# Convolution history kept as a partial sum, and decay and gate comparisons that read PSUM

## The chip, the cores and the metric

The kernel runs on one core of a Trainium2 chip. The metric is the device time of one execution in microseconds (us). Three runs of the kernel before took 3788.0, 3789.68 and 3792.01 us; the median, 3789.68 us, is what the prediction is about. Below, PE is the matrix engine (TensorE), PEld its weight loads, DVE is VectorE, ACT is ScalarE, POOL is GpSimd and SP the engine that issues most DMAs. SBUF is the working memory, PSUM the accumulators that PE writes; POOL reads SBUF alone here.

## The reference

One decoder layer over 1024 tokens of width 1024. Cut to what matters:

```
proj = rms_norm(x) @ w_in      -> z, xbc, dt, u, v, q, gates
xbc  = silu(conv(xbc))         # causal depthwise convolution, 4 taps, 1536 channels
       conv: y[t] = b + w3*x[t] + w2*x[t-1] + w1*x[t-2] + w0*x[t-3]
branch A (SSD), per chunk of 128 tokens and head:
       L[s,l] = exp(a_cs[l] - a_cs[s]) where l >= s, else 0
       y_diag = (L * (B C^T)) applied to x*dt ;  a state is carried from chunk to chunk
branches B (spatial gate) and C (attention into 256 memory tokens), merged by gates, out projection
x = x + PEER(rms_norm(x)):
       per token 8 heads choose 16 of 16384 experts (i, j), i, j < 128, with softmax gates
       out = sum over chosen e of gate_e * gelu(u_e . x) * v_e
```

## The kernel before

**Blocks.** Tokens are worked through in three blocks of 256, 256 and 512 (`BLOCKS`). `mixer(b, ...)` does the three branches of a block. For blocks 0 and 1 the chosen experts' rows are gathered from memory row by row (`gathered`): per token tile and slot one indirect DMA issued by POOL (L793), and one DVE operation of 128x1024 (L803 for u, L810 for v). For block 2 all experts are computed densely (`dense`), with a matrix of gates, one value per token and expert, that `gate_matrix` builds beforehand. The gathers run all through the kernel beside the other work. Most matmuls take three passes (L187 to L189, `mm3`) on a high and a low half of each operand; `unit` fetches a weight tile, ACT makes its high half (L160), and POOL, or DVE for some, makes the low half by a subtraction of two SBUF tiles (L161).

**Convolution (`conv_tile`).** Features stand on the 128 partitions, tokens along the free dimension; there are 12 tiles a block. PE leaves the projection in a PSUM tile (`mm_ps`, four buffers). ACT writes tap 3 and the bias to the tile `ac` in SBUF (L297). For each of the other taps DVE does two operations: L300 adds the shifted projection, read from PSUM, to `ac`; L302 adds, on the first 3, 2 or 1 tokens, the last tokens of the block before, kept in SBUF in `hist`. Then ACT copies the block's last three tokens from PSUM to `hist` (L304) and applies Silu (L306); after L304 the PSUM tile is free. PE turns some results to token order (L310, into `tp_ps`, two buffers).

**Decay product (`chunk_a`).** Per chunk PE makes two B C^T products in one `tp_ps` tile (L413), ACT copies them to `cbs` in SBUF (L416, one buffer), PE and ACT make four tiles of exponentials (L419 to L427), and DVE multiplies each by `cbs` (L428).

**Gate matrix (`gate_matrix`).** For each of four token tiles, PE turns expert numbers j, gates and expert numbers i into one `tp_ps` tile (L817); ACT copies j and the gates to `tr` in fp32 (L819) and i to `ti` in bf16 (L821). Then, 32 times for four tokens each (called a quad below; 128 in all): DVE compares `iota4` with i into `eq` in bf16 (L827) and `iota` with j into `oj` in fp32 (L829), both 128x512; POOL multiplies three tokens of `eq` by the gate (L833, 128x384), ACT the fourth (L836); PE multiplies the two (L839, four matmuls); ACT copies the result out (L841); each eight quads SP writes a stage to memory (L843). `eq`, `oj`, `oi` and the activations of `dense` share 22 buffers (`d2`).

**Order.** The program is written in one order; a scheduler lays the instructions of each engine out by priorities, and each engine runs its own list in order. Some gathers are tied to weight units by `pace`.

Of the kernel before, what the change touches and what calls it, by code (L numbers as in the profile page):

```python
# [21 lines left out]
T = 512  # L22
TT = T // P
BLOCKS = ((0, 256), (256, 256), (512, 512))
# [5 lines left out]
NXBC = 12  # L30
# [12 lines left out]
POOL_G = 3  # L43
# [15 lines left out]
def layer_kernel(ctx, tc, a, out_d):  # L59
    nc = tc.nc  # L60
# [28 lines left out]
    def d2(dp, dt=F32):  # L89
        return dp.tile([P, T], dt, tag="d2", name="d2", bufs=NDP)  # L90
# [4 lines left out]
    def col(v, n):  # L95
        return v[:, n:n + 1]
# [30 lines left out]
    a_neg = const.tile([P, 16], F32, name="a_neg")  # L127
    nc.scalar.activation(a_neg, rows[:, RW_ALOG:RW_ALOG + 16], AF.Exp)
    nc.vector.tensor_scalar(a_neg, a_neg, -1.0, None, op0=ALU.mult)
    hist = const.tile([P, NXBC, 3], F32, name="hist")  # L130
    nc.vector.memset(hist, 0.0)
    prev = const.tile([P, D], F32, name="prev")

    x2_d = drm.tile([SEQ, D], F32, name="x2_d")
# [154 lines left out]
                                           op0=ALU.mult, op1=ALU.subtract)  # L289
        return hT  # L290

    def conv_tile(f, hT, dst, turned):
        T = hT[0].shape[-1]
        ps = feat(a["win_a"][FA_XBC + f], hT)
        cw = PK_CONVW + f * 4
        ac = t2()[:, :T]
        nc.scalar.activation(ac, ps, AF.Identity, bias=col(pk, PK_CONVB + f), scale=col(pk, cw + 3))  # L297
        for j in range(3):
            s = 3 - j
            nc.vector.scalar_tensor_tensor(ac[:, s:T], ps[:, 0:T - s], col(pk, cw + j), ac[:, s:T],  # L300
                                           op0=ALU.mult, op1=ALU.add)
            nc.vector.scalar_tensor_tensor(ac[:, 0:s], hist[:, f, j:3], col(pk, cw + j), ac[:, 0:s],  # L302
                                           op0=ALU.mult, op1=ALU.add)
        nc.scalar.copy(hist[:, f, :], ps[:, T - 3:T])  # L304
        src = ac if dst is None else dst
        nc.scalar.activation(src, ac, AF.Silu)  # L306
        if turned is not None:
            tp = tp_ps()
            for c in range(T // P):
                nc.tensor.transpose(tp[:, c * P:(c + 1) * P], src[:, c * P:(c + 1) * P], ident)  # L310
            nc.scalar.copy(turned, tp[:, :T].rearrange("p (c d) -> p c d", c=T // P))
# [4 lines left out]
    def mixer(b, hT, lmt=None):  # L316
# [7 lines left out]

        xy = b16()[:, :TT * D].rearrange("p (c d) -> p c d", c=TT)
        for f in range(4):
            conv_tile(f, hT, None, xy[:, :, f * P:(f + 1) * P])
            yield "conv"

        bc = a16()  # L330
# [12 lines left out]
            mm3(fps[0:16, :], hi[:, k, :], lo[:, k, :], hT[0][:, k, :], hT[1][:, k, :], k == 0, k == KD - 1)  # L343
        dtT = tT()
        nc.scalar.copy(dtT[0:16, :], fps[0:16, :])
        conv_tile(4, hT, None, xy[:, :, 4 * P:5 * P])
        yield "conv"
        dps = tp_ps()
        for t in range(TT):
# [20 lines left out]
        nc.vector.scalar_tensor_tensor(dt, dr, 0.0, pol, op0=ALU.max, op1=ALU.add)  # L370
        adt = s64()
        nc.vector.tensor_tensor(adt, dt, a_neg[:, None, :].to_broadcast([P, TT, 16]), op=ALU.mult)
        conv_tile(8, hT, bcT[:, 0, :], btok[:, :, 0:P])
        yield "conv"
        cps = tp_ps()
        adt_f = adt.rearrange("p c h -> p (c h)")
# [12 lines left out]
        nc.scalar.activation(cdec, cps[:, 64:64 + NS].rearrange("p (c h) -> p c h", c=TT), AF.Exp)  # L389

        for f in (9, 10, 11):
            conv_tile(f, hT, bcT[:, f - 8, :], btok[:, :, (f - 8) * P:(f - 7) * P] if f < 10 else None)
            yield "conv"
        for f in (5, 6, 7):
            conv_tile(f, hT, None, xy[:, :, f * P:(f + 1) * P])
            yield "conv"

        def gate(n, f):
# [10 lines left out]
        def chunk_a(c):  # L409
            cb = tp_ps()  # L410
            cs = slice(c * P, (c + 1) * P)
            for g in range(2):
                nc.tensor.matmul(cb[:, g * P:(g + 1) * P], lhsT=bcT[:, g, cs], rhs=bcT[:, 2 + g, cs],  # L413
                                 start=True, stop=True)
            cbs = sml.tile([P, 2, P], F32, tag="cbs", name="cbs", bufs=1)
            nc.scalar.copy(cbs, cb[:, 0:256].rearrange("p (g l) -> p g l", g=2))  # L416
            for x in range(4):
                seg = mm_ps()
                nc.tensor.matmul(seg, lhsT=identb, rhs=maskb[:, None, :].to_broadcast([P, 4, P]), start=True, stop=False)  # L419
                for j in range(4):  # L420
                    h = x * 4 + j
                    nc.tensor.matmul(seg[:, j * P:(j + 1) * P], lhsT=adt[:, c, h:h + 1].to_broadcast([P, P]),
                                     rhs=triu, start=False, stop=(j == 3))
                lm = lmt[:, (c + 1) % 2, x]
                for j in range(4):
                    h = x * 4 + j
                    nc.scalar.activation(lm[:, j, :], seg[:, j * P:(j + 1) * P], AF.Exp, bias=nacs[:, c, h:h + 1])  # L427
                nc.vector.tensor_tensor(lm, lm, cbs[:, x // 2, None, :].to_broadcast([P, 4, P]), op=ALU.mult)  # L428
# [385 lines left out]
    def gate_matrix(t, i_f, j_f, gt, dp):  # L814
        tp = tp_ps()
        for n, v in enumerate((j_f, gt, i_f)):
            nc.tensor.transpose(tp[:, n * P:(n + 1) * P], v, ident)  # L817
        tr = sml.tile([P, 2, P], F32, tag="cbs", name="tr", bufs=1)
        nc.scalar.copy(tr, tp[:, 0:256].rearrange("p (n t) -> p n t", n=2))  # L819
        ti = sml.tile([P, P], BF16, tag="tri", name="tri", bufs=1)  # L820
        nc.scalar.copy(ti, tp[:, 256:384])  # L821
        for s in range(P // STG):
            stage = a16().rearrange("p (i t) -> p i t", t=STG)
            for q in range(STG // 4):
                m0 = s * STG + q * 4
                eq = d2(dp, BF16).rearrange("p (i t) -> p i t", t=4)
                nc.vector.tensor_tensor(eq, iota4, ti[:, None, m0:m0 + 4].to_broadcast([P, P, 4]), op=ALU.is_equal)  # L827
                oj = d2(dp).rearrange("p (t i) -> p t i", t=4)
                nc.vector.tensor_tensor(oj, iota[:, None, :].to_broadcast([P, 4, P]),  # L829
                                        tr[:, 0, m0:m0 + 4, None].to_broadcast([P, 4, P]), op=ALU.is_equal)  # L830
                oi = d2(dp).rearrange("p (t i) -> p t i", t=4)
                e4 = eq.rearrange("p i t -> p t i")
                nc.gpsimd.tensor_tensor(oi[:, 0:POOL_G], e4[:, 0:POOL_G],  # L833
                                        tr[:, 1, m0:m0 + POOL_G, None].to_broadcast([P, POOL_G, P]), op=ALU.mult)
                for u in range(POOL_G, 4):
                    nc.scalar.activation(oi[:, u], e4[:, u], AF.Copy, scale=tr[:, 1, m0 + u:m0 + u + 1])  # L836
                ps = mm_ps()
                for u in range(4):
                    nc.tensor.matmul(ps[:, u * P:(u + 1) * P], lhsT=oj[:, u, :], rhs=oi[:, u, :],  # L839
                                     start=True, stop=True)  # L840
                nc.scalar.copy(stage[:, :, q * 4:q * 4 + 4].rearrange("p i t -> p t i"),  # L841
                               ps.rearrange("p (t i) -> p t i", t=4))
            nc.sync.dma_start(g_d[t * (P // STG) + s], stage.rearrange("p i t -> p (i t)"))  # L843
# [243 lines left out]
```

## Time and profile before

| | |
|---|---|
| median of three runs | 3789.68 us |
| the profiled execution | 3783.22 us |
| its span, first to last instruction | 3781.2 us |
| PE busy | 3319.3 us, 88% of the span |
| DVE busy | 3014.4 us, 80% |
| POOL busy | 2579.4 us, 68% |
| ACT busy | 1472.5 us, 39% |
| data moved by DMA | 1012.82 MB, 268 GB/s mean |

The profile comes from one execution. The busy shares are means over stages with different limits. The stages, read from where lines first and last run: block 0's mixer to about 430 us; block 1's to 900 us beside the routing (choice of experts) of block 0; block 2's from 900 us beside block 1's routing, with the convolution up to 1340 us; the gate matrix from 2323 to 2556 us; the dense part from there to the end.

### The profile page before, as it was taken

What the parts mean: (1) busy time and instruction counts of PE and PEld (TensorE: products, weight loads), DVE (VectorE), ACT (ScalarE), POOL (GpSimd) and SP (SyncE); (2) the same over time, 40 slices, a digit from 0 to 9 for tenths busy, and PEclk for the clock granted to TensorE, in tenths of its full rate; (3) what the DMA queues carried; (4) which work ended last, traced back from release to release, by engine and by line L of the source; (5) the groups of instructions that cost most, each with busy time, mean ns of one, the idle gap of its engine ahead of it and who ended that gap; (6) DMA issues with size and microseconds to landing.
All of it is one profiled execution on the core that took longest, in us unless ns stands there. A gap on an engine that the chain in (4) does not pass through costs nothing. (4 is left out here: it accounts for less than half of the span.)

```text
span 3781.2 us, 49410 instructions
## 1 busy us (share of the span) xinstructions
PE 3319.3 (88%) x16928; PEld 2794.8 (74%) x16928; DVE 3014.4 (80%) x5393; ACT 1472.5 (39%) x2239; POOL 2579.4 (68%) x1867
## 2 busy tenths in 40 slices
PE   7899977888877759999989886778999999999998
PEld 6689867778756647777767675666888888888776
DVE  3622489753699999878999998995888888888888
ACT  5454555443434433423332333872222223222222
POOL 6478757688776767688777666664676666666664
PEclk9899988899988879999999997998999999999999
DMA  5255555477787768999998763358999999999997
GB/s 192 69 170 193 185 178 183 158 239 257 278 315 240 240 212 304 345 352 348 339 364 275 250 227 130 156 200 305 342 343 351 328 355 333 339 347 346 332 337 256
DMA packets 353436, 1012.82 MB, mean 268 GB/s; under 512 B 32544, under 2 KB 117920, under 8 KB 350752
## 3 DMA queue, kind: packets, MB, share of 16 engines
q0 software_dynamic: 147456, 536.94, 38.8%
q1 hardware_dynamic: 205728, 472.72, 36.7%
q8 instruction: 134, 2.20, 0.2%
q14 instruction: 118, 0.97, 0.1%
HBM read 945.56 MB, written 63.96 MB: 267 GB/s over the span
## 5 line engine op out<-in xcount | busy, mean ns | idle before, releaser
L161 POOL TENSOR_TENSOR wlo<-raw,whi 128x1024 fp32r<-128x1024 f32 x491 | 1179.3, 2406 | 483.0 <-ACT whi L160 360.8
L160 ACT CAST whi<-raw 128x1024 fp32r<-128x1024 f32 (+1 forms) x623 | 648.1, 1044 | 1163.5 <-issue 364.2
L187 PE MATMUL mm_ps<-a,whi 128*128 128x256 f32 (+2 forms) x2552 | 865.3, 343 | 102.1 <-ACT hist L304 33.8
L189 PE MATMUL mm_ps<-a,wlo 128*128 128x256 f32 (+2 forms) x2552 | 858.3, 339 | 37.7 <-POOL wlo L161 37.4
L188 PE MATMUL mm_ps<-a,whi 128*128 128x256 f32 (+2 forms) x2552 | 860.1, 338 | 3.2 <-DVE a L161 1.9
L793 POOL DMA_INDIRECT g<-in_v_dram,eid x512 | 529.1, 1033 | 304.9 <-DVE row_ps L810 104.7
L803 DVE SCALAR_TENSOR_TENSOR g<-g,row_ps 128x1024 f32<-128x1024 f32 x512 | 606.7, 1211 | 103.9 <-DMA g<-in_u_dram,eid 90.8
L793 POOL DMA_INDIRECT g<-in_u_dram,eid x512 | 529.4, 1034 | 215.4 <-DVE g L803 91.0
L810 DVE SCALAR_TENSOR_TENSOR row_ps<-g,dots,row_ps 128x1024 f32<-128x1024 f32 x512 | 655.7, 1281 | 7.9 <-ACT row_ps L780 1.2
L187 PEld LDWEIGHTS mm_ps<-a,whi 128*128 128x128 f32 (+1 forms) x2552 | 509.0, 201 | 158.4 <-ACT hist L304 36.0
L189 PEld LDWEIGHTS mm_ps<-a,wlo 128*128 128x128 f32 (+1 forms) x2552 | 507.7, 200 | 90.3 <-POOL wlo L161 48.2
L188 PEld LDWEIGHTS mm_ps<-a,whi 128*128 128x128 f32 (+1 forms) x2552 | 511.0, 200 | 47.1 <-DVE a L161 3.4
L188 PE MATMUL mm_ps<-wlo,d 128*128 128x512 f32 x1024 | 406.3, 397 | 0.2 <-POOL wlo L161 0.2
L189 PE MATMUL mm_ps<-whi,d 128*128 128x512 f32 x1024 | 403.5, 396 | 0.0
L187 PE MATMUL mm_ps<-whi,d 128*128 128x512 f32 x1024 | 384.0, 397 | 18.9 <-ACT d L160 16.8
L187 PE MATMUL tp_ps<-a,whi 128*128 128x512 f32 x768 | 302.4, 394 | 10.4 <-ACT d L927 10.4
L189 PE MATMUL tp_ps<-a,wlo 128*128 128x512 f32 x768 | 302.7, 394 | 3.6 <-POOL wlo L161 2.0
L188 PE MATMUL tp_ps<-a,whi 128*128 128x512 f32 x768 | 302.1, 393 | 0.0
L161 DVE TENSOR_TENSOR wlo<-raw,whi 128x1024 fp32r<-128x1024 f32 x132 | 183.8, 1393 | 77.3 <-ACT whi L160 66.3
L187 PEld LDWEIGHTS mm_ps<-whi,d 128*128 128x128 f32 x1024 | 192.9, 188 | 66.7 <-ACT d L160 17.1
L188 PEld LDWEIGHTS mm_ps<-wlo,d 128*128 128x128 f32 x1024 | 193.0, 188 | 47.1 <-POOL wlo L161 0.6
L189 PEld LDWEIGHTS mm_ps<-whi,d 128*128 128x128 f32 x1024 | 193.0, 188 | 46.2
(261 smaller groups left out, 5149.1 us busy)
## 6 DMA issues: line engine op xcount, KB each, us to landing
raw<-in_win_a_dram SPq DMA_DIRECT2D x156, 512.0 KB
raw<-in_uT_a_dram SPq DMA_DIRECT2D x128, 512.0 KB
raw<-in_v_b_dram SPq DMA_DIRECT2D x128, 512.0 KB
raw<-in_br_a_dram SPq DMA_DIRECT2D x72, 512.0 KB
g_d<-a SPq DMA_DIRECT2D x16, 2048.0 KB
a<-g_d SPq DMA_DIRECT2D x32, 1024.0 KB
raw<-in_win_b_dram SPq DMA_DIRECT2D x48, 512.0 KB
raw<-in_pq_a_dram SPq DMA_DIRECT2D x48, 512.0 KB
```

Of the source, the lines that this page charges most:

```text
L160: return (nc.scalar.copy(hi, src), (eng or nc.vector).tensor_tensor(lo, src, hi.bitcast(F32), op=ALU.subtract))
L161: (eng or nc.vector).tensor_tensor(lo, src, hi.bitcast(F32), op=ALU.subtract))
L187: nc.tensor.matmul(ps, lhsT=l_hi, rhs=r_hi, start=start, stop=False)
L188: nc.tensor.matmul(ps, lhsT=l_hi, rhs=r_lo, start=False, stop=False)
L189: nc.tensor.matmul(ps, lhsT=l_lo, rhs=r_hi, start=False, stop=stop)
L793: nc.gpsimd.indirect_dma_start(out=g, out_offset=None, in_=a[table], in_offset=bass.IndirectOffsetOnAxis(ap=eid[:, k:k + 1], axis=0))
L803: nc.vector.scalar_tensor_tensor(g, g, 1.0, xn, op0=ALU.mult, op1=ALU.mult, accum_out=col(w, k))
L810: nc.vector.scalar_tensor_tensor(acc, g, col(w, k), acc, op0=ALU.mult, op1=ALU.add)
```

## The change

There are three edits.

1. `hist` goes. Instead of the last three tokens, `carry` keeps what they will add to the next block's first three tokens, with the bias. It is computed from the PSUM tile by three small DVE operations (not in the last block): `tensor_scalar` on 3 tokens, and two operations on 2 and 1. The next block adds it by one operation on `ac[:, 0:3]` that reads PSUM and `carry`; it recomputes the token's own tap 3. ACT's L304 goes. In block 0 there is nothing to add.
2. `cbs` is no copy any more: DVE's multiplication reads the PSUM tile of the two products itself.
3. Both comparisons of the gate matrix read i and j from the PSUM tile of the transposes and compare with the fp32 `iota`; `eq` stays bf16, but lies token by token. Only the gates are copied to SBUF (`tr`, now two buffers).

```
-    hist = const.tile([P, NXBC, 3], F32, name="hist")
-    nc.vector.memset(hist, 0.0)
+    carry = const.tile([P, NXBC, 3], F32, name="carry")
...
         nc.scalar.activation(ac, ps, AF.Identity, bias=col(pk, PK_CONVB + f), scale=col(pk, cw + 3))
+        if b > 0:
+            nc.vector.scalar_tensor_tensor(ac[:, 0:3], ps[:, 0:3], col(pk, cw + 3), carry[:, f, :],
+                                           op0=ALU.mult, op1=ALU.add)
         for j in range(3):
             s = 3 - j
             nc.vector.scalar_tensor_tensor(ac[:, s:T], ps[:, 0:T - s], col(pk, cw + j), ac[:, s:T],
                                            op0=ALU.mult, op1=ALU.add)
-            nc.vector.scalar_tensor_tensor(ac[:, 0:s], hist[:, f, j:3], col(pk, cw + j), ac[:, 0:s],
-                                           op0=ALU.mult, op1=ALU.add)
-        nc.scalar.copy(hist[:, f, :], ps[:, T - 3:T])
+        if b + 1 < len(BLOCKS):
+            nc.vector.tensor_scalar(carry[:, f, :], ps[:, T - 3:T], col(pk, cw), col(pk, PK_CONVB + f),
+                                    op0=ALU.mult, op1=ALU.add)
+            for j in (1, 2):
+                nc.vector.scalar_tensor_tensor(carry[:, f, 0:3 - j], ps[:, T - 3 + j:T], col(pk, cw + j),
+                                               carry[:, f, 0:3 - j], op0=ALU.mult, op1=ALU.add)
...
-            cbs = sml.tile([P, 2, P], F32, tag="cbs", name="cbs", bufs=1)
-            nc.scalar.copy(cbs, cb[:, 0:256].rearrange("p (g l) -> p g l", g=2))
+            cbs = cb[:, 0:256].rearrange("p (g l) -> p g l", g=2)
...
-        tr = sml.tile([P, 2, P], F32, tag="cbs", name="tr", bufs=1)
-        nc.scalar.copy(tr, tp[:, 0:256].rearrange("p (n t) -> p n t", n=2))
-        ti = sml.tile([P, P], BF16, tag="tri", name="tri", bufs=1)
-        nc.scalar.copy(ti, tp[:, 256:384])
+        tr = sml.tile([P, P], F32, tag="tr", name="tr", bufs=2)
+        nc.scalar.copy(tr, tp[:, P:2 * P])
...
-                eq = d2(dp, BF16).rearrange("p (i t) -> p i t", t=4)
-                nc.vector.tensor_tensor(eq, iota4, ti[:, None, m0:m0 + 4].to_broadcast([P, P, 4]), op=ALU.is_equal)
+                eq = d2(dp, BF16).rearrange("p (t i) -> p t i", t=4)
                 oj = d2(dp).rearrange("p (t i) -> p t i", t=4)
-                nc.vector.tensor_tensor(oj, iota[:, None, :].to_broadcast([P, 4, P]),
-                                        tr[:, 0, m0:m0 + 4, None].to_broadcast([P, 4, P]), op=ALU.is_equal)
+                for one_hot, n in ((eq, 2), (oj, 0)):
+                    nc.vector.tensor_tensor(one_hot, iota[:, None, :].to_broadcast([P, 4, P]),
+                                            tp[:, n * P + m0:n * P + m0 + 4, None].to_broadcast([P, 4, P]),
+                                            op=ALU.is_equal)
```

**How the order moves.** First the start of one convolution tile of block 1 on DVE (the fifth, `t_5189` before and `t_5172` after), among routing (L694 to L759 before) and gathers (L803 before, L808 after). Before:

```order
L300 SCALAR_TENSOR_TENSOR t_5189<-mm_ps,pk,t_5189 128x253
L302 SCALAR_TENSOR_TENSOR t_5189<-hist,pk,t_5189 128x3
L712 MAX gate<-b_4655 128x8
L362 TENSOR_TENSOR a_4834<-a_4834 128x32
L713 MAX_INDEX bp<-gate,b_4655 128x8
L715 MATCH_REPLACE c_5106<-gate,b_4655 128x112
L803 SCALAR_TENSOR_TENSOR g_27878,dots<-g_27878,row_ps 128x1024
L300 SCALAR_TENSOR_TENSOR t_5189<-mm_ps,pk,t_5189 128x254
L302 SCALAR_TENSOR_TENSOR t_5189<-hist,pk,t_5189 128x2
```

The same place after:

```order
L299 SCALAR_TENSOR_TENSOR t_5172<-mm_ps,pk,carry 128x3
L303 SCALAR_TENSOR_TENSOR t_5172<-mm_ps,pk,t_5172 128x253
L717 MAX gate<-b_4638 128x8
L368 TENSOR_TENSOR a_4817<-a_4817 128x32
L718 MAX_INDEX bp<-gate,b_4638 128x8
L720 MATCH_REPLACE c_5089<-gate,b_4638 128x112
L808 SCALAR_TENSOR_TENSOR g_27805,dots<-g_27805,row_ps 128x1024
L303 SCALAR_TENSOR_TENSOR t_5172<-mm_ps,pk,t_5172 128x254
```

The L302 rows are gone and one row with `carry` stands ahead; the rest keeps its order. The end of the same tile on DVE, before:

```order
L716 MAX gate<-c_5106 128x8
L803 SCALAR_TENSOR_TENSOR g_27884,dots<-g_27884,row_ps 128x1024
L300 SCALAR_TENSOR_TENSOR t_5189<-mm_ps,pk,t_5189 128x255
L302 SCALAR_TENSOR_TENSOR t_5189<-hist,pk,t_5189 128x1
L716 MAX gate<-c_5112 128x8
```

And after:

```order
L721 MAX gate<-c_5089 128x8
L808 SCALAR_TENSOR_TENSOR g_27811,dots<-g_27811,row_ps 128x1024
L303 SCALAR_TENSOR_TENSOR t_5172<-mm_ps,pk,t_5172 128x255
L306 TENSOR_SCALAR carry<-mm_ps,pk 128x3
L721 MAX gate<-c_5095 128x8
L372 SCALAR_TENSOR_TENSOR a_4817<-a_4817 128x32
L722 MAX_INDEX bp<-gate,c_5089 128x8
L808 SCALAR_TENSOR_TENSOR g_27814,dots<-g_27814,row_ps 128x1024
L309 SCALAR_TENSOR_TENSOR carry<-mm_ps,pk,carry 128x2
L722 MAX_INDEX bp<-gate,c_5095 128x8
L372 SCALAR_TENSOR_TENSOR a_4817<-a_4817 128x32
L309 SCALAR_TENSOR_TENSOR carry<-mm_ps,pk,carry 128x1
```

The three operations that make `carry`, the last of which frees the PSUM tile, stand among routing and gather rows. Last, DVE at the start of the gate matrix (`d` are `eq`, `oj` in turn), before:

```order
L827 TENSOR_TENSOR d_18274<-iota_100,tri 128x512
L829 TENSOR_TENSOR d_18276<-iota,tr 128x512
L827 TENSOR_TENSOR d_18287<-iota_100,tri 128x512
L829 TENSOR_TENSOR d_18289<-iota,tr 128x512
L803 SCALAR_TENSOR_TENSOR g_29560,dots<-g_29560,row_ps 128x1024
```

And after:

```order
L832 TENSOR_TENSOR d_18207<-iota,tp_ps 128x512
L832 TENSOR_TENSOR d_18208<-iota,tp_ps 128x512
L832 TENSOR_TENSOR d_18220<-iota,tp_ps 128x512
L832 TENSOR_TENSOR d_18221<-iota,tp_ps 128x512
L808 SCALAR_TENSOR_TENSOR g_29487,dots<-g_29487,row_ps 128x1024
```

The sequence is the same with other operands. Over the whole list POOL issues 549 gathers ahead of the first product of the gate matrix in both kernels; of the rest, five stood among its last products before, and stand right behind the last one after.

## Rows read from the trace of the kernel before

**Rows 1.** Busy time by stretch: PE, PEld, DVE, ACT, POOL, granted clock, DMA share, GB/s.

```profile
0.00:430.00 430.00, 376.71 (x2619) 347.14 (x2620) 170.30 (x262) 221.04 (x381) 292.45 (x153) 0.96 0.48 155
430.00:900.00 470.00, 378.78 (x2465) 348.31 (x2464) 328.38 (x891) 235.00 (x365) 336.76 (x215) 0.88 0.60 202
900.00:1340.00 440.00, 349.33 (x1879) 299.24 (x1879) 377.16 (x869) 185.53 (x287) 320.67 (x240) 0.89 0.77 265
2323.00:2556.00 233.00, 161.47 (x1081) 144.19 (x1081) 211.22 (x283) 171.08 (x267) 157.63 (x139) 0.89 0.44 177
2556.00:3781.00 1225.00, 1191.64 (x5136) 965.68 (x5136) 1031.86 (x1249) 347.21 (x458) 760.31 (x575) 0.99 0.92 332
```

**Rows 2.** Lines L300 and L302: shortest, median, longest in ns.

```profile
L300 DVE SCALAR_TENSOR_TENSOR t<-mm_ps,pk,t x108: 452/481/749, 80.7 to 1339.8; 128x253 f32<-128x253 f32 x24, 128x254 f32<-128x254 f32 x24, 128x255 f32<-128x255 f32 x24, 128x509 f32<-128x509 f32 x12
L302 DVE SCALAR_TENSOR_TENSOR t<-hist,pk,t x108: 201/211/4218, 81.1 to 1340.5; 128x3 f32<-128x3 f32 x36, 128x2 f32<-128x2 f32 x36, 128x1 f32<-128x1 f32 x36
```

**Rows 3.** One tile of block 1 on DVE, in order of time.

```profile
530.59 0.47 DVE L300 SCALAR_TENSOR_TENSOR t<-mm_ps,pk,t 128x253 f32<-128x253 f32 x1
530.98 4.22 DVE L302 SCALAR_TENSOR_TENSOR t<-hist,pk,t 128x3 f32<-128x3 f32 x1
```

**Rows 4.** POOL at that time.

```profile
530.45 4.72 POOL L161 TENSOR_TENSOR wlo<-raw,whi 128x1024 fp32r<-128x1024 f32 x2
```

**Rows 5.** Line L302 by stretch: busy time and count.

```profile
0.00:430.00 430.00, 26.81 (x36) 0.96 0.48 155
430.00:900.00 470.00, 30.27 (x36) 0.88 0.60 202
900.00:1340.00 440.00, 34.77 (x35) 0.89 0.77 265
```

**Rows 6.** Waits: who waited for whom, us in total, times, longest.

```profile
ACT hist L304 <- DVE t L302: 112.6, 28, 8.7
PE tp_ps L310 <- ACT t L306: 43.8, 18, 9.1
PE mm_ps L187 <- ACT hist L304: 33.8, 10, 5.7
```

**Rows 7.** Gate matrix, lines: count, shortest, median, longest in ns.

```profile
L827 DVE TENSOR_TENSOR d<-iota,tri x128: 410/1046/2601, 2327.9 to 2548.4; 128x512 bf16<-128x512 bf16 x128
L833 POOL TENSOR_TENSOR d<-d,tr x128: 817/1144/1284, 2330.6 to 2549.6; 128x384 f32<-128x384 bf16 x128
```

**Rows 8.** One quad of the gate matrix in order of time.

```profile
2399.42 1.14 POOL L833 TENSOR_TENSOR d<-d,tr 128x384 f32<-128x384 bf16 x1 [0.43 <-DVE d L827]
2399.80 1.04 DVE L827 TENSOR_TENSOR d<-iota,tri 128x512 bf16<-128x512 bf16 x1
2400.77 0.68 DVE L829 TENSOR_TENSOR d<-iota,tr 128x512 f32<-128x512 f32 x1
...
2400.99 1.15 POOL L833 TENSOR_TENSOR d<-d,tr 128x384 f32<-128x384 bf16 x1 [0.43 <-DVE d L827]
...
2401.37 1.05 DVE L827 TENSOR_TENSOR d<-iota,tri 128x512 bf16<-128x512 bf16 x1
```

**Rows 9.** ACT there, where its work had piled up.

```profile
2391.93 0.43 ACT L836 ACTIVATE d<-d,tr 128x128 f32<-128x128 bf16 x1
2392.22 1.06 ACT L841 COPY a<-mm_ps 128x512 f32<-128x512 f32 x1
2393.04 0.43 ACT L836 ACTIVATE d<-d,tr 128x128 f32<-128x128 bf16 x1
```

**Rows 10.** DVE lines by shape: count, busy us, mean ns, idle before.

```profile
L428 DVE TENSOR_TENSOR b<-b,cbs 128x512 f32<-128x512 f32 x32 | 40.0, 1284 | 24.6 <-ACT cbs L416 14.9 <-ACT b L427 9.7
L912 DVE TENSOR_TENSOR a<-a,mm_ps 128x512 f32<-128x512 f32 x176 | 113.9, 680 | 22.1 <-PE mm_ps L189 16.7 <-issue 5.2
L161 DVE TENSOR_TENSOR a<-tp_ps,a 128x512 fp32r<-128x512 f32 x8 | 5.4, 687 | 4.1 <-ACT a L160 4.1
L803 DVE SCALAR_TENSOR_TENSOR g<-g,row_ps 128x1024 f32<-128x1024 f32 x512 | 606.7, 1211 | 103.9 <-DMA g<-in_u_dram,eid 90.8 <-issue 11.9 <-ACT row_ps L780 0.8
```

More of the change, by code (lines that the diff above doesn't have):

```diff
@@ L290, in x_turn, with conv_tile @@
         return hT
-    def conv_tile(f, hT, dst, turned):
+    def conv_tile(b, f, hT, dst, turned):
         T = hT[0].shape[-1]
@@ L326, in mixer @@
         for f in range(4):
-            conv_tile(f, hT, None, xy[:, :, f * P:(f + 1) * P])
+            conv_tile(b, f, hT, None, xy[:, :, f * P:(f + 1) * P])
             yield "conv"
@@ L345, in mixer @@
         nc.scalar.copy(dtT[0:16, :], fps[0:16, :])
-        conv_tile(4, hT, None, xy[:, :, 4 * P:5 * P])
+        conv_tile(b, 4, hT, None, xy[:, :, 4 * P:5 * P])
         yield "conv"
@@ L372, in mixer @@
         nc.vector.tensor_tensor(adt, dt, a_neg[:, None, :].to_broadcast([P, TT, 16]), op=ALU.mult)
-        conv_tile(8, hT, bcT[:, 0, :], btok[:, :, 0:P])
+        conv_tile(b, 8, hT, bcT[:, 0, :], btok[:, :, 0:P])
         yield "conv"
@@ L391, in mixer @@
         for f in (9, 10, 11):
-            conv_tile(f, hT, bcT[:, f - 8, :], btok[:, :, (f - 8) * P:(f - 7) * P] if f < 10 else None)
+            conv_tile(b, f, hT, bcT[:, f - 8, :], btok[:, :, (f - 8) * P:(f - 7) * P] if f < 10 else None)
             yield "conv"
         for f in (5, 6, 7):
-            conv_tile(f, hT, None, xy[:, :, f * P:(f + 1) * P])
+            conv_tile(b, f, hT, None, xy[:, :, f * P:(f + 1) * P])
             yield "conv"
@@ L825, in gate_matrix @@
                 m0 = s * STG + q * 4
-                eq = d2(dp, BF16).rearrange("p (i t) -> p i t", t=4)
-                nc.vector.tensor_tensor(eq, iota4, ti[:, None, m0:m0 + 4].to_broadcast([P, P, 4]), op=ALU.is_equal)
+                eq = d2(dp, BF16).rearrange("p (t i) -> p t i", t=4)
                 oj = d2(dp).rearrange("p (t i) -> p t i", t=4)
-                nc.vector.tensor_tensor(oj, iota[:, None, :].to_broadcast([P, 4, P]),
-                                        tr[:, 0, m0:m0 + 4, None].to_broadcast([P, 4, P]), op=ALU.is_equal)
+                for one_hot, n in ((eq, 2), (oj, 0)):
+                    nc.vector.tensor_tensor(one_hot, iota[:, None, :].to_broadcast([P, 4, P]),
+                                            tp[:, n * P + m0:n * P + m0 + 4, None].to_broadcast([P, 4, P]),
+                                            op=ALU.is_equal)
                 oi = d2(dp).rearrange("p (t i) -> p t i", t=4)
-                e4 = eq.rearrange("p i t -> p t i")
-                nc.gpsimd.tensor_tensor(oi[:, 0:POOL_G], e4[:, 0:POOL_G],
-                                        tr[:, 1, m0:m0 + POOL_G, None].to_broadcast([P, POOL_G, P]), op=ALU.mult)
+                nc.gpsimd.tensor_tensor(oi[:, 0:POOL_G], eq[:, 0:POOL_G],
+                                        tr[:, m0:m0 + POOL_G, None].to_broadcast([P, POOL_G, P]), op=ALU.mult)
                 for u in range(POOL_G, 4):
-                    nc.scalar.activation(oi[:, u], e4[:, u], AF.Copy, scale=tr[:, 1, m0 + u:m0 + u + 1])
+                    nc.scalar.activation(oi[:, u], eq[:, u], AF.Copy, scale=tr[:, m0 + u:m0 + u + 1])
                 ps = mm_ps()
```

## The prediction

> **What bounds the kernel now.** I read the busy time by stretch first [rows 1]. In the last stretch PE is busy 1191.6 of 1225 us, so the dense part is PE's, and the change touches nothing in it. The other stretches have no such owner. In blocks 1 and 2 (430 to 1340 us) PE is busy 81% and 79%, DVE 70% and 86%, and in the gate matrix DVE is busy 211 of 233 us. There the question is which wait ends last, so the next views were single lines and the order of time.
>
> The convolution's line L302 is the odd one. It works on 3, 2 or 1 tokens and takes 0.211 us in the median, but up to 4.218 us, while L300, on some 250 to 510 tokens, never takes more than 0.749 us [rows 2]. In the order of time the 4.22 us operation starts at 530.98 and ends at 535.20; POOL began two low-half subtractions at 530.45 that end at 535.17 [rows 3, 4]. L302 reads two SBUF tiles (`hist`, `ac`), L300 one and PSUM. So what is paid is a wait for POOL inside the operation, and it falls on DVE operations whose tensor inputs both lie in SBUF. Over the three blocks L302 is busy 26.8 + 30.3 + 34.8 = 91.9 us [rows 5]; 107 times 0.211 would be 22.6, so 69 us are waiting.
>
> The gate matrix shows the same. L827 takes 0.410 us at best and 1.046 in the median, POOL's product 0.817 at best and 1.144 in the median [rows 7]. In one quad POOL starts at 2399.42; L827 starts at 2399.80, while POOL runs, and ends at 2400.84, 0.28 us after POOL's end at 2400.56; the next POOL product can only then start, at 2400.99 [rows 8]. The quad's period is 2400.99 - 2399.42 = 1.57 us: POOL's product, the rest of the comparison that it held up, and 0.15 us of hand-over. 128 quads make 201 of the stage's 233 us. Nobody is the bottleneck; two engines take turns.
>
> **The gate matrix.** After the change neither comparison has two SBUF tensors. Each costs what a 128x512 operation with a PSUM operand costs: 0.680 us (L912) to 0.687 us (L161) [rows 10]; successive ones overlap, as L829 starts at 2400.77 and its successor at 2401.37, 0.60 us later, for 0.68 us of length [rows 8]. So DVE needs 1.20 to 1.37 us a quad. ACT needs 1.11 us (2391.93 to 2393.04, product and copy without a pause) [rows 9], and POOL 0.82 to 1.14 us, now without DVE in its way. The largest is DVE. I take 1.25 us, near the lower end, since DVE runs up to four quads ahead through the shared buffers (22 less 8 activations, three a quad) and so waits for nobody. Gain: 128 x (1.57 - 1.25) = 41 us; ends 128 x 0.20 = 26 and 128 x 0.37 = 47.
>
> The comparison `eq` loses something too: its shortest record, 0.410 us, against 0.68 for the fp32 one [rows 7, 8], which is 0.27 us x 128 = 35 us of DVE time that an undisturbed bf16 comparison would have saved. It is not lost here, since the median was 1.046. [...]
>
> [...]
>
> What else moves there: the transposes' PSUM tile is now held until a token tile's last comparison, so those of tiles 2 and 3 wait on PE for a buffer; with DVE four quads ahead that is covered, and without this cover it costs at most 4 x 1.25 us twice, 10 us. ACT's copies of i and j go, which have slack. Five gathers, at 1.211 us of DVE each [rows 10], pass from the stage's end to the start of the dense part: 0 to 6 us there, taken as 2, since DVE is busy 84% of it.
>
> **The convolution.** Small operations: 107 or 108 of L302 go (at 0.211 us, 23 us); 36 + 36 for `carry` in blocks 0 and 1 and 12 + 12 to add it in blocks 1 and 2 come, 96 in all. No row shows a PSUM operation on three tokens by DVE; bounds are L302's 0.201 and L300's 0.452 us [rows 2], 19 to 43 us. I take 0.21, the row nearest in size: 20 us, so the work is about equal. What goes is the 69 us of waiting, in shares of 19, 23 and 27 us by block.
>
> How much of it lies on the path? ACT stood 112.6 us in 28 waits for L302, PE 33.8 us for L304, which frees the PSUM tile, and 43.8 us for Silu behind it [rows 6]; so the convolution's chain does hold PE up. But in block 0 DVE is busy only 40% [rows 1], so I count a fifth there, 4 us. In blocks 1 and 2 DVE also does routing and gathers, and many of those small operations read two SBUF tiles: with POOL still subtracting, the next one can inherit the wait. I count half, 11 and 14 us. Sum 29; ends 0 (all inherited) and 69.
>
> The PSUM tile is freed by the last `carry` operation, behind other DVE rows, where it was freed by ACT behind the last L302. Queued behind the waiting PE matmul is the rest of PE's list. Cost: L302's turn in the queue is replaced by some five to eight small rows more, about 2 us a tile for 24 tiles at worst, 48 us; four PSUM buffers cover it and I take nothing. In block 2 no `carry` is made and the tile comes free earlier.
>
> **The decay product.** L428 is busy 40.0 us; 32 times 0.68 would be 22, so 18 us go from DVE, and ACT's copy with it [rows 10]. Against it, the product's PSUM tile, one of two, is held through four multiplications, at least 4 x 0.68 = 2.7 us for each of 8 chunks, 22 us. Both ends are small and partly hidden; I take 0.
>
> **The sum.** 41 + 29 - 2 = 68 us. The profiled execution took 3783.22 us (span 3781.2 and 2 us around it) and would take 3715; the median of the runs shown lies 6.5 us above it, so the prediction is 3722 us. The dense part follows the gate matrix and is PE's, so what is won ahead of it moves the end. The likeliest case by itself covers 3695 to 3745.
>
> **Rivals.**
>
> - *The wait only moves.* In blocks 1 and 2 the next operation with two SBUF inputs waits for the same POOL subtraction. For it: POOL is busy 72% and 73% there [rows 1], and DVE's list is full of such operations. Against: PE and ACT waited for this chain and not for routing. Then only the gate matrix gains: 3790 - 41 + 2 = 3751 us. Chance 0.22.
> - *All waits come out.* 41 + 69 + 18 - 2 = 126, 3664 us. For it: DVE is busy 86% in block 2, so its time counts nearly in full; against, the slack in block 0. Chance 0.13.
> - *Slower: comparisons from PSUM run long.* Both read one PSUM element for 128 results, a pattern that no row has. If each took the 1.05 us that L827 takes now, with the 0.08 us overlap, DVE would need 1.94 us a quad: 128 x 0.37 = 47 us lost, less 29 gained, plus 2: 3810 us. It decides the sign from a period of 1.57 + 27/128 = 1.78 us, 0.89 us a comparison. Against: L829 reads the same pattern from SBUF at 0.68, and L912 reads PSUM at 0.68. Chance 0.06.
> - *The change doesn't do what it says.* The PSUM tiles held longer (48 + 22 + 10 us by the bounds above) eat the gain of 68: about 3790 us. Against: four buffers, and PE's waits for two-buffer tiles are few. Chance 0.04.
>
> **How the numbers follow.** Likeliest 0.55, rivals 0.22, 0.13, 0.06 and 0.04. 0.2% of 3790 is 7.6 us, about what a measurement can tell from no change. Faster by more: 0.55 + 0.22 + 0.13 = 0.90; same 0.04; slower 0.06. The range takes in the first rival with its gate gain at the lower end of 26 us (3766) and the second: 3664 to 3768 us.
>
> **What would show it.** Right: comparisons at 0.68 us with little scatter, POOL's product near 0.82, a gate stage of 185 to 195 us, the `carry` rows all near 0.2 us, and ACT's waits for DVE ahead of Silu clearly under 112 us. The first rival shows as routing lines with two SBUF inputs (the candidates' sums, L702 and L705) getting longer while the convolution's get shorter. Wrong would be a quad above 1.4 us, or PE waiting for `carry` or for a `tp_ps` buffer.

## The result and the profile after

The changed kernel took 3728.61 us in the median of four runs (3719.16 to 3742.35), the kernel before 3790.35 on the same chip: ratio 0.984, 95% interval 0.9805 to 0.9876, 62 us less where 68 were forecast. A second series of the same kernel gave 3729.77 us beside 3783.2 of before (0.9863, 0.9846 to 0.9879), 53 us less. In parentheses stand, here and below, the ratio to before and its 95% interval. The profiled execution is the longest of the first four, 3742.35 us with a span of 3740.6; that of the second series took 3722.83 us. Where the two differ, both are given.

First the single lines after, as in [rows 2, 7, 10]: shortest, median and longest duration in ns, then first and last start.

```profile
L299 DVE SCALAR_TENSOR_TENSOR t<-mm_ps,pk,carry x24: 196/208/245, 450.5 to 1289.8; 128x3 f32<-128x3 f32 x24
L306 DVE TENSOR_SCALAR carry<-mm_ps,pk x24: 265/272/276, 84.1 to 664.8; 128x3 f32<-128x3 f32 x24
L309 DVE SCALAR_TENSOR_TENSOR carry<-mm_ps,pk,carry x48: 118/212/223, 84.4 to 666.2; 128x2 f32<-128x2 f32 x24, 128x1 f32<-128x1 f32 x24
L433 DVE TENSOR_TENSOR b<-b,tp_ps x32: 662/680/690, 134.9 to 1391.4; 128x512 f32<-128x512 f32 x32
L832 DVE TENSOR_TENSOR d<-iota,tp_ps x256: 677/681/690, 2295.0 to 2490.1; 128x512 bf16<-128x512 f32 x128
L836 POOL TENSOR_TENSOR d<-d,tr x128: 826/827/837, 2297.3 to 2490.4; 128x384 f32<-128x384 bf16 x128
```

The longest record is the number to read. Of the old line of small rows it was 4218 ns; of its successors none exceeds 276. The decay product went from a mean of 1284 to a median of 680 with a longest of 690, the comparisons and POOL's product each stay within 13 ns. All waiting inside these operations is gone.

The small carry rows keep the PSUM tile long enough to be waited for only twice. In the waits of the whole execution (us in total, times, longest), ahead of Silu (L312, counted at its table load), for its output (L316), and in the gate matrix for a stage tile:

```profile
ACT L312 <- DVE t L303: 76.4, 16, 11.0
PE tp_ps L316 <- ACT t L312: 35.2, 14, 5.2
ACT a L844 <- DMA g_d<-a: 12.7, 6, 3.8
```

ACT's wait was 112.6 us, though ahead of another operation, and PE's 43.8 [rows 6]; with the Silu operations themselves ACT's is now 86.6 us in 22 waits. The third row was 0.3 us before: ACT waits for the DMA that empties a stage tile.

Busy time by stretch, columns as in [rows 1]: block 2's convolution, the gate matrix and the dense part.

```profile
883.00:1297.00 414.00, 346.94 (x1862) 296.86 (x1863) 350.97 (x861) 185.31 (x280) 315.25 (x236) 0.91 0.79 276
2297.00:2498.00 201.00, 159.47 (x1078) 146.52 (x1078) 160.07 (x264) 154.87 (x259) 106.10 (x129) 0.87 0.44 178
2498.00:3741.00 1243.00, 1195.50 (x5136) 968.85 (x5136) 1041.34 (x1259) 347.72 (x459) 765.70 (x581) 0.98 0.92 329
```

The convolution's stretch is 26 us shorter as these windows are cut (22 by the table below, from block 1's last Silu to block 2's), the gate matrix 23 by the table (the window of before begins 7 us ahead of the first product). In the gate matrix nobody is busy throughout any more: DVE 160 of 201 us, ACT 155, POOL 106. So DVE at 1.25 us a quad is not what sets its length. The dense part's window is 18 us longer in this execution with 4 us more of PE; by the table it is 16 us longer, and 5 in the second series.

Where each kernel stands at the same place is read from the first or last start of one line there. The column of before is in us; the others are differences to it.

| place (line in before) | before | after | again | conv_only | decay_only | gate_only | early_free |
|---|---|---|---|---|---|---|---|
| block 1, last Silu (L306) | 688.2 | -21.5 | -21.9 | -23.3 | -5.5 | -1.1 | -21.7 |
| block 2, last Silu (L306) | 1342.2 | -43.4 | -47.9 | -44.8 | -8.7 | -1.0 | -45.6 |
| block 2, last decay product (L428) | 1453.1 | -61.7 | -66.3 | -61.2 | -17.4 | -1.1 | -64.0 |
| block 2, last output projection (L634) | 1906.7 | -53.4 | -59.4 | -57.0 | -26.7 | -4.9 | -55.4 |
| gate matrix, first product (L833) | 2330.6 | -33.3 | -40.0 | -31.1 | -7.0 | -5.2 | -36.2 |
| gate matrix, last copy (L841) | 2552.9 | -56.4 | -64.7 | -31.0 | -7.2 | -33.0 | -93.6 |
| dense part, last sum (L912) | 3765.2 | -40.5 | -60.1 | -21.9 | -3.0 | -24.3 | -81.8 |

Negative numbers are earlier. Read down the column "again": 66 us are won by the end of block 2's chunks, 26 are given back before the gate matrix, which wins 25, and the dense part gives back 5. The differences between one row and the next are the terms of the sum.

### The profile page after: what moved, and what is told of

It reads as the page before. It is cut to its first block, busy times and chain, and to the rows that moved or that the text cites. A ratio compares the mean times of both kernels' runs of the same rounds, so it can differ in the third digit from the quotient of the medians.

```text
span 3740.6 us, 49425 instructions
## 1 busy us (share of the span) xinstructions
PE 3312.7 (89%) x16928; PEld 2792.3 (75%) x16928; DVE 2918.0 (78%) x5380; ACT 1454.8 (39%) x2192; POOL 2533.8 (68%) x1867
## 5 line engine op out<-in xcount | busy, mean ns | idle before, releaser
L808 DVE SCALAR_TENSOR_TENSOR g<-g,row_ps 128x1024 f32<-128x1024 f32 x512 | 607.7, 1213 | 120.9 <-DMA g<-in_u_dram,eid 116.5
```

The source lines that it names most:

```text
L808: nc.vector.scalar_tensor_tensor(g, g, 1.0, xn, op0=ALU.mult, op1=ALU.mult, accum_out=col(w, k))
```

## The experiments

**Each edit alone, and the change again.** Edit numbers are those of the section on the change.

```
gate_only:   before with edit 3 alone
conv_only:   before with edit 1 alone
decay_only:  before with edit 2 alone
after_again: the changed kernel, no edit
```

> The kernel before with the third edit alone (both comparisons read PSUM). Theory: the comparisons no longer wait, but the transposes' PSUM tile is held to the last comparison of a token tile, so the last transposes come 32 quads later and the 16 KB tile of the routing, which could serve as a second stage buffer, comes free 32 quads later; until then eight quads take an ACT copy of each plus the stage's DMA, 15.4 us. First comparison to last copy: 200 to 205 us (226 before); total 24 us less, 3766 us. Rival (the forecast's arithmetic, 1.25 us a quad all through): 185 us, total 3749 us. Rival (the gate stage was short only by the company of the other edits): under 10 us gained.

> The kernel before with the first edit alone (carry). Theory: 40 us gained when block 2's convolution ends, since no convolution row waits for POOL; about half is given back in the routing of block 2, where other operations with two SBUF inputs wait instead; total 20 to 30 us less, 3760 to 3770 us. Rival (the wait only moves): less than 8 us in the end. Rival (all waits come out): 60 us or more.

> The kernel before with the second edit alone (decay product from PSUM). Theory: the multiplications at 0.68 us instead of a mean of 1.28, 18 us less DVE time, and ACT's 29 us of waits for the single buffer of the copy go; 10 to 18 us ahead after block 2's chunks, 5 to 15 in the end, 3775 to 3785 us. Rival (the held tp_ps tile costs what the multiplication wins): no difference over 3 us at the end of the chunks.

> The changed kernel once more, for a second trace of it. Theory: gate stage again 200 to 205 us, every time, since it is set by buffers; the spread of the runs seen (3719 to 3742 us) lies in the routing of block 2 and the dense part, where DVE's waits for POOL depend on how the two lists meet; median 3715 to 3740. Rival: the gate stage varies by 10 us or more between traces.

Measured against 3783.2 us of before: gate_only 3759.05 (0.995, 0.993 to 0.997), conv_only 3754.78 (0.9921, 0.9904 to 0.9937), decay_only 3779.8 (0.9993, 0.9983 to 1.0003). That is 24 + 28 + 3 = 56 us beside 53 for the whole, so within their intervals the edits add up. The convolution's 28 us are near the 29 forecast, and the decay product's 3 us can't be told from the 0 forecast, though 5 to 15 were expected ahead of its run. The gate matrix is worth 24, not 41. Its stage, from the first comparison to the end of the last copy, took 226.0 us in before, 199.2 in gate_only (200 to 205 expected), 202.6 and 201.3 in the two traces of after.

**Why the gate matrix falls short.** ACT after, with the DMA issues of SP's queue (SPq), in order of time: start, duration, and in brackets the idle time before it.

```profile
2329.49 0.40 ACT L839 ACTIVATE d<-d,tr 128x128 f32<-128x128 bf16 x1
2329.60 0.83 POOL L836 TENSOR_TENSOR d<-d,tr 128x384 f32<-128x384 bf16 x1 [0.37 <-DVE d L832]
2329.67 0.33 SPq L846 DMA_DIRECT2D g_d<-a  x1
2330.77 0.40 ACT L839 ACTIVATE d<-d,tr 128x128 f32<-128x128 bf16 x1 [0.88 <-PE mm_ps L842]
...
2334.33 0.40 ACT L839 ACTIVATE d<-d,tr 128x128 f32<-128x128 bf16 x1 [0.80 <-DVE d L832]
...
2336.00 1.87 ACT L844 COPY a<-mm_ps 128x512 f32<-128x512 f32 x2 [1.26 <-DMA g_d<-a]
```

A stage tile is full at 2329.67 and its DMA issued; until 2336.00 ACT makes no copy (L844), only products, and then it copies what has piled up. The same pause stands ahead of the copies at 2320.56, 2350.51, 2367.58, 2382.88 and 2397.63: 77.1 us from the first to the last for 40 quads, 1.93 us a quad. The prediction had named a quad above 1.4 us as a sign that it is wrong, and for these 40 quads that sign is there. There is one stage tile where two were meant. The other is still held by the routing's results, which the transposes read. PE's transposes, kernel before and kernel after:

```profile
L817 PE MATMUL tp_ps<-ident,a x12: 270/272/329, 2321.8 to 2387.8; 128*128 128x128 f32 x12
```

```profile
L822 PE MATMUL tp_ps<-ident,a x12: 271/273/330, 2289.0 to 2408.7; 128*128 128x128 f32 x12
```

The last of the twelve starts 57 us after the first product before, 111 us after it now. On PE's list nine stood at the front and three behind 28 quads; now there are six, three behind 28 and three behind 60, since a token tile's PSUM tile is free only when its comparisons are done. Once the routing's tile is free, ACT sets the pace without a pause:

```profile
2429.16 0.51 ACT L839 ACTIVATE d<-d,tr 128x128 f32<-128x128 bf16 x1
2429.44 1.17 ACT L844 COPY a<-mm_ps 128x512 f32<-128x512 f32 x1
...
2430.29 0.51 ACT L839 ACTIVATE d<-d,tr 128x128 f32<-128x128 bf16 x1
```

That is 1.13 us a quad. If this is the cause, freeing the routing's tile early must give the loss back; and in before, where the second buffer came earlier and a quad took 1.57 us, nearly nothing.

```
early_free (after) and early_free_before (before):
     r = routing(xnT, a16(), beside=beside)
...
+    held_r = []
+    for v in r:
+        c = d2(dp).rearrange("p (t s) -> p t s", t=TT)
+        nc.scalar.copy(c, v)
+        held_r.append(c)
...
-        gate_matrix(t, r[0][:, t], r[1][:, t], r[2][:, t], dp)
+        gate_matrix(t, held_r[0][:, t], held_r[1][:, t], held_r[2][:, t], dp)
```

> The changed kernel, with one thing more: i, j and gates are copied by ACT from the routing's 16 KB tile into three of the 22 shared 2 KB buffers ahead of the gate matrix, so that the 16 KB tile is free from the start and serves as a second stage buffer. Theory (the missing part of the gate gain is the stage buffer): no ACT wait for the stage's DMA, 1.13 to 1.25 us a quad all through, first product to last copy 160 to 170 us (198 in the changed kernel), total 3690 to 3705 us. Rival (the stage is bound by ACT's copy or by fewer quads in flight): 190 us or more, total 3720 to 3735 us.

> The same copies in the kernel before, which holds no PSUM tile: there the 16 KB tile came free after 28 quads anyway. Theory: first product to last copy 208 to 215 us (222 before), since a quad stays at 1.57 us while POOL and the comparison take turns; total 3770 to 3780 us. Rival (the stage buffer alone explains the gate stage, the comparisons' operands little): 190 us or less.

Measured against 3783.64 us: early_free 3695.18 (0.9763, 0.9745 to 0.978), the fastest of all kernels here; early_free_before 3779.09 (0.9975, 0.9962 to 0.9988). From first product to last copy the stage takes 164.9 us where after took 199.2 and 197.6; in before the same copies bring 222.3 to 215.9, just above the 208 to 215 expected. In early_free no copy of ACT waits for a DMA any more, while the last transposes still come late, at 2375.3, 81 us after the first product. The quads of early_free:

```profile
2359.76 4.88 DVE L832 TENSOR_TENSOR d<-iota,tp_ps 128x512 f32<-128x512 f32 x8
...
2360.02 0.83 POOL L836 TENSOR_TENSOR d<-d,tr 128x384 f32<-128x384 bf16 x1 [0.37 <-DVE d L832]
...
2361.22 0.83 POOL L836 TENSOR_TENSOR d<-d,tr 128x384 f32<-128x384 bf16 x1 [0.37 <-DVE d L832]
```

DVE works without a pause, eight comparisons in 4.88 us, and a quad takes 1.20 us: the regime that the prediction described, and near its 1.25. It was right for 128 quads with two stage tiles. The edit itself prevented that, by 33 to 34 us. Against the changed kernel these copies of 3 x 0.62 us bring 35 us, 3729.77 to 3695.18, each from its own comparison with before.

**Which of the two comparisons it was.** Both operands were moved to PSUM. Starting from early_free, one comparison at a time is put back.

```
eq_from_sbuf:
+        ti = sml.tile([P, P], BF16, tag="tri", name="tri", bufs=2)
+        nc.scalar.copy(ti, tp[:, 2 * P:3 * P])
...
+                eq = d2(dp, BF16).rearrange("p (i t) -> p i t", t=4)
+                nc.vector.tensor_tensor(eq, iota4, ti[:, None, m0:m0 + 4].to_broadcast([P, P, 4]), op=ALU.is_equal)
...
oj_from_sbuf:
+        tj = sml.tile([P, P], F32, tag="trj", name="tj", bufs=1)
+        nc.scalar.copy(tj, tp[:, 0:P])
...
+                for one_hot, js in ((eq, tp[:, 2 * P + m0:2 * P + m0 + 4, None]), (oj, tj[:, m0:m0 + 4, None])):
```

> As early_free, but the comparison with i reads a bf16 copy in SBUF again, as in the kernel before (j still from PSUM). Theory (a DVE operation with two SBUF tensors and POOL's product shut each other out): this comparison back to about 1 us in the median, though 0.41 us undisturbed, POOL's product to 1.14, a quad 1.5 us, first product to last copy 200 to 210 us. Rival (PSUM operands gained by something else, as fewer copies): 160 to 175 us, since the bf16 comparison is then the shorter one.

> The mirror of eq_from_sbuf: as early_free, but the comparison with j (oj, fp32) reads its second operand from an SBUF copy tj, and only the one with i (eq) reads PSUM. In eq_from_sbuf, where eq read SBUF and oj read PSUM, POOL's product took 0.83 us and the gate stage (first product to last copy) 168 us, 3 more than in early_free. Theory A: it was oj, whose two fp32 SBUF tensors lie beside POOL's product, that lengthened the product from 0.83 to 1.14 us in the kernel before. Then POOL's product is back near 1.1 us here, oj near 0.9 to 1.0, and the stage takes 190 to 215 us, the kernel 3715 to 3745. Theory B: one comparison with two SBUF inputs is harmless whichever it is, since only two of them in a row leave DVE no time to absorb the wait. Then POOL's product stays at 0.83 us, the stage takes 165 to 175 us, the kernel 3695 to 3712.

Measured: eq_from_sbuf 3706.47 us against 3783.64 (0.979, 0.9771 to 0.9808), stage 167.9 us; oj_from_sbuf 3706.82 against 3784.58 (0.9808, 0.9789 to 0.9827), stage 172.3. In time each run came out by its second theory: either comparison alone costs the stage little, 3 and 7 us (the whole kernel 11 us each; where the rest of that lies was not tried). In the rows each first theory was right about one thing: eq is held up again, though less than the 1 us expected and without POOL's product going to 1.14, and POOL's product is long again beside oj, though oj itself is not. Lines of eq_from_sbuf (L832 is eq, L834 oj, L838 POOL's product):

```profile
L832 DVE TENSOR_TENSOR d<-iota,tri x128: 412/736/2222, 2289.0 to 2455.9; 128x512 bf16<-128x512 bf16 x128
L834 DVE TENSOR_TENSOR d<-iota,tp_ps x128: 672/675/684, 2289.4 to 2456.5; 128x512 f32<-128x512 f32 x128
L838 POOL TENSOR_TENSOR d<-d,tr x128: 826/831/838, 2292.4 to 2456.7; 128x384 f32<-128x384 bf16 x128
```

Lines of oj_from_sbuf (eq and oj share L834; `tj` marks oj):

```profile
L834 DVE TENSOR_TENSOR d<-iota,tj x128: 675/712/719, 2292.0 to 2458.9; 128x512 f32<-128x512 f32 x128
L837 POOL TENSOR_TENSOR d<-d,tr x128: 834/1150/1240, 2293.5 to 2459.1; 128x384 f32<-128x384 bf16 x128
```

Two different harms had been one in the kernel before. eq from SBUF is itself held up, 0.736 us against 0.412 at best, and leaves POOL alone. oj from SBUF is not held up, 0.712 us against 0.675 at best, but lengthens POOL's product from 0.83 to 1.150, the 1.144 of before [rows 7]. The order of starts tells them apart, here in eq_from_sbuf:

```profile
2381.23 0.83 POOL L838 TENSOR_TENSOR d<-d,tr 128x384 f32<-128x384 bf16 x1 [0.43 <-DVE d L832]
2381.61 0.74 DVE L832 TENSOR_TENSOR d<-iota,tri 128x512 bf16<-128x512 bf16 x1
...
2382.27 0.68 DVE L834 TENSOR_TENSOR d<-iota,tp_ps 128x512 f32<-128x512 f32 x1
2382.49 0.83 POOL L838 TENSOR_TENSOR d<-d,tr 128x384 f32<-128x384 bf16 x1 [0.43 <-DVE d L832]
```

POOL starts first, eq starts inside it and ends at 2382.35, 0.29 us after POOL's end at 2382.06, as in [rows 8] (0.28). A quad takes 1.26 us. In oj_from_sbuf it is oj that starts first, 0.25 us ahead of POOL, whose four products then last 4.85 us:

```profile
2379.69 0.72 DVE L834 TENSOR_TENSOR d<-iota,tj 128x512 f32<-128x512 f32 x1
...
2379.94 4.85 POOL L837 TENSOR_TENSOR d<-d,tr 128x384 f32<-128x384 bf16 x4
```

With both from SBUF, oj makes POOL end 1.150 - 0.831 = 0.32 us later, and eq waits for that later end: 1.26 + 0.32 = 1.58, an estimate from the two runs beside the 1.57 of before [rows 8]. In these rows of the gate matrix the one that starts first keeps its length and the other is held up, in both directions: POOL's product stays at 0.83 us and eq ends 0.29 us after its end; oj stays at 0.71 us and POOL's product becomes 0.32 us longer.

**Whether the wait for ACT's place in line was the convolution's cost.** A rival to waits inside L302: that the tile was freed by another engine, behind a semaphore and ACT's list.

```
hist_copy_on_dve (before):
-        nc.scalar.copy(hist[:, f, :], ps[:, T - 3:T])
+        nc.vector.tensor_copy(hist[:, f, :], ps[:, T - 3:T])
```

> The kernel before with L304, the copy of the last three tokens, on DVE instead of ACT, and all else left. Theory (the time is lost inside L302, in its wait for POOL, not in ACT standing in line): L302 busy 80 to 100 us again, less than a third of the convolution edit's 45 us gained at the end of block 2's convolution. Rival (ACT's place in line was the cost): 30 us or more gained there. Beside that the order is shuffled as much as by the convolution edit; if the stretch from block 2's output to the first gate product (424 us before, 443 to 450 in the kernels with another order) is long again, the loss there comes with a new order, not with the edit.

Measured 3801.26 us against 3783.64 (1.0045, 1.0029 to 1.0061), 18 us longer. Block 2's last Silu comes 9.6 us later than in before, where the rival wanted it 30 us or more earlier. The line of small rows is as it was, busy 93.3 us (92.1 in before):

```profile
L302 DVE SCALAR_TENSOR_TENSOR t<-hist,pk,t x108: 201/212/3162, 80.7 to 1350.3; 128x3 f32<-128x3 f32 x36, 128x2 f32<-128x2 f32 x36, 128x1 f32<-128x1 f32 x36
```

So taking ACT out of the release of the tile gains nothing while the two SBUF operands stay, and of the two theories the one of the operands is left. What makes this kernel 18 us longer was not tried; the order of DVE's rows changed with it.

**Where 20 us go between block 2's output projection and the gate matrix.** In the table, before and gate_only take 424 us for it; after, conv_only, decay_only and early_free take 443 to 450. The stretch is the routing of the last block. Busy time, before and then after, columns as in [rows 1]:

```profile
1907.00:2330.00 423.00, 355.82 (x1513) 285.44 (x1513) 407.33 (x1184) 130.38 (x176) 290.22 (x214) 0.91 0.74 255
```

```profile
1853.00:2297.00 444.00, 356.49 (x1510) 284.10 (x1510) 426.97 (x1185) 131.58 (x176) 291.76 (x215) 0.91 0.71 246
```

DVE sets this stretch, busy 96% of it, and the same number of instructions takes it 20 us more. Most of that lies in the small rows between SBUF tiles that take the chosen numbers apart (L722 to L734 of before): their durations sum to 36.9 us in before and 54.9 after, some longer and some shorter. Two that grew (busy us, mean ns; L733 and L734 of before are L738 and L739 after):

```profile
L733 DVE SCALAR_TENSOR_TENSOR pf<-pf 128x64 f32<-128x64 f32 x8 | 4.0, 497 | 0.0
L734 DVE TENSOR_TENSOR ab<-pf 128x64 bf16<-128x64 f32 x8 | 5.0, 628 | 0.0
```

```profile
L738 DVE SCALAR_TENSOR_TENSOR pf<-pf 128x64 f32<-128x64 f32 x8 | 12.2, 1531 | 0.0
L739 DVE TENSOR_TENSOR ab<-pf 128x64 bf16<-128x64 f32 x8 | 8.7, 1092 | 0.0
```

A mean of 1531 ns for 64 elements a partition, where the shortest of the eight rows takes 198 ns and the longest 4959, is a wait again. Is the stretch longer because a kernel comes to it earlier, or because its rows stand in another order? The next kernel comes earlier with DVE's, POOL's, PE's and SP's lists unchanged.

```
cbs_two_buffers (before):
-            cbs = sml.tile([P, 2, P], F32, tag="cbs", name="cbs", bufs=1)
+            cbs = sml.tile([P, 2, P], F32, tag="cb2", name="cbs", bufs=2)
```

> The kernel before, with two buffers for cbs instead of one; the copy and the multiplication by two SBUF tiles stay. DVE, PE, POOL and SP keep their lists row for row, on ACT the copy of one chunk moves up by two exponentials in two places. In the kernel before ACT waited 28.9 us five times for the buffer and DVE 14.9 us four times for the copy. This asks whether the stretch from block 2's early part to the gate matrix gets longer because a kernel comes to it earlier (theory A) or because its rows stand in another order (theory B): all kernels with the convolution or the decay edit needed 444 to 450 us from the end of block 1's output projection of the routing stretch (out2) to the first gate product, against 424 before. If the two buffers bring out2 forward by 5 us or more, A expects the stretch to lengthen by most of that (430 us or more) and B expects it to stay at 422 to 426. If they bring nothing forward (under 3 us), nothing follows, and the total is within 0.3% of before's.

Measured 3780.63 us (0.9991, 0.9979 to 1.0002). It comes to the stretch 7.1 us earlier and to the gate matrix 8.5 us earlier:

```profile
1899.60:2322.00 422.40, 352.18 (x1513) 282.26 (x1513) 407.17 (x1185) 130.70 (x177) 289.59 (x214) 0.93 0.74 256
```

DVE's 407 us are those of before. So arriving earlier is, at 7 us, not enough to lengthen the stretch. Nor is a new order as such: hist_copy_on_dve has its rows there in another order too and takes 426.8 us. But it is no chance of one execution: the sum of the small rows is 36.8 to 36.9 us in before, gate_only, cbs_two_buffers and early_free_before, and 54.8 to 55.2 in both traces of after, in early_free and in the two kernels made from it, which come to the stretch 53 to 59 us earlier. What is left is the particular way in which DVE's and POOL's rows meet in a kernel with a shorter convolution or decay product. Whether its list or the 50 us make it was not settled.

## Why the prediction was right, and where it was not

The time and the sign came out by the named mechanism. Of the terms, the gate matrix was taken too large, and the convolution's size was right by luck.

- *The mechanism* (a row between SBUF tiles waits for POOL, one with a PSUM operand does not): shown, by the single lines after, by both halves of the comparison pair and by hist_copy_on_dve. Counted in the trace of before: of 27 L302 rows that start inside a two-tensor operation of POOL, 25 last over 0.3 us longer than the shortest of their shape, of 23 that start inside a gather's issue, 9, and of 57 that start while POOL is idle, one; of L300's 24 inside such an operation, none; of the 34 `carry` rows after, none. "Tensor inputs both lie in SBUF" is too narrow, though. A routing row of before with one SBUF input waits as well:

```profile
L728 DVE TENSOR_SCALAR pf<-pf x24: 164/180/3009, 511.2 to 2300.0; 128x32 f32<-128x32 f32 x16, 128x64 f32<-128x64 f32 x8
```

Its longest ends at 2099.72, 0.06 us after the end of a POOL subtraction that began 0.55 us behind it. So the rows that could take a wait over were more than the prediction counted.
- *Gate matrix, 41 us*: 23 to 25 came (28 in the stage of gate_only, 24 in its whole time), and the stage of 185 to 195 us that the prediction gave as a sign took 201. The step that failed is "with DVE four quads ahead that is covered, and without this cover it costs at most ... 10 us". The prediction weighed what waits for the transposes in PE's list, and not what their input holds: the routing's tile is the second stage tile. It cost 33 to 34 us by early_free. The period of 1.25 us itself was right (1.20 there), and so was POOL's 0.83.
- *Comparisons from PSUM*: 0.681 us as taken. The rival of 1.05 us a comparison fell. In eq_from_sbuf oj takes 0.675 us from PSUM, in the kernel before 0.68 from SBUF [rows 8], so reading PSUM didn't lengthen the fp32 comparison.
- *Convolution, 29 us*: 28.4 alone. That the number fits is luck, for it is no half of the waits. When block 2's convolution ends, conv_only is 45 us ahead, two thirds of the 69, since most of the waits did lie on the path there. It is 61 ahead at the last decay product, where no convolution row stands any more; in that stretch DVE is busy 13 us less, 8 of them since six gather rows fewer stand in it. Then 30 us are lost again up to the gate matrix, and 9 more by the end. So the likeliest case and two rivals were each partly true: "all waits come out" in good part up to 1450 us, "the wait only moves" from 1900 us on. It does not move to the two rows that the prediction named: in the last block's routing L702 (L707 after) has a mean of 849 ns for 755, L705 (L710 after) of 794 for 982, together 3 us less. It moves to the rows L722 to L734 behind them, 18 us more. DVE's busy time over the whole execution tells the same: the changed lines last about 129 us less, but DVE is busy only 96 less, 3014.4 to 2918.0 us.
- *Tile held by `carry`*: "four PSUM buffers cover it" held, 8.4 us of PE's waits in two pieces.
- *Decay product, 0*: 3.4 us, with an interval that includes 0. Its 18 us were won (17.4 by block 2's last decay product, 26.7 by its output projection), and all but 7 lost by the gate matrix.
- *Dense part, 2 us lost*: about 5 us in the second series and 16 in the first profiled execution. But conv_only, hist_copy_on_dve and early_free_before are 8 to 9 us longer than before there too, without the gate matrix's new order of gathers, so one trace each can't tell the 2 us. Both traces of after have the same gate stage (197.6 and 199.2 us), so nearly all of the 19.5 us between these two executions lies outside it, 11 here and 7 ahead of the gate matrix. What makes them was not tried.

## What to carry to other kernels

A DVE operation whose longest record is many times its median, with its inputs in SBUF and POOL busy beside it, may be waiting inside (L302: 4218 ns against 211); see in the order of time whether it ends just behind a POOL operation. Here one PSUM operand removed the wait (no small row of the convolution above 276 ns after), but the time counts only as far as the rows behind it don't take the wait over, so read the gain at the stages' ends and not in the line. When an operand stays in PSUM instead of being copied, ask what its producer reads, since that too is freed later; here a copy of 2 us gave back 34. And two engines that take turns may need only one of them freed: with either comparison alone the stage lost 3 and 7 us of what both had gained.

## What the runs showed of the hardware that was not expected

- A bf16 comparison of two SBUF tiles and an fp32 one of the same shape hurt in opposite directions: the first, which starts inside POOL's product, waits (0.736 us against 0.412 at best), the second, which starts ahead of it, makes POOL's product longer (1.150 against 0.831 us). It is not the type that decides: L302 is fp32 too, starts inside POOL's subtractions and waits, up to 4.218 us against 0.201 at best [rows 2, 3, 4].
- In two records a waiting DVE row got no turn between POOL operations that followed each other closely. L302's 4.22 us span two subtractions [rows 3, 4]. The longest L738 after starts inside a gather's issue, 0.32 us ahead of POOL's next operation, and lasts 4.96 us, until 0.09 us after the end of the third POOL operation behind that issue (the first and third are shown). So here, outside the gate matrix, the row with the earlier recorded start was not the one that went first.

```profile
2117.91 4.96 DVE L738 SCALAR_TENSOR_TENSOR pf<-pf 128x64 f32<-128x64 f32 x1
```

```profile
2118.23 2.02 POOL L746 TENSOR_TENSOR a<-a,topi 128x1024 bf16<-128x1024 bf16 x1
...
2120.39 2.39 POOL L160 TENSOR_TENSOR wlo<-raw,whi 128x1024 fp32r<-128x1024 f32 x1
```

- The granted clock of PE in the gate matrix was 0.97 of full speed in early_free, where PE was busy 157.4 of 167 us (row below), and 0.87 after, where it was busy 159.5 of 201. After, it was 0.78 up to 2410 us, the part with the pauses for the stage tile (PE busy 75.0 of 113 us), and 1.00 from there on (84.5 of 88 us). PE's busy time differs by 2 us of 159, so the stage didn't get its 34 us from there.

```profile
2294.00:2461.00 167.00, 157.39 (x1078) 135.99 (x1078) 158.56 (x265) 153.64 (x259) 106.18 (x129) 0.97 0.52 214
```
